# A hybrid decoder layer on one core: arithmetic moved off GpSimd, and another order of the branches S5, gMLP and SSD

## The chip, the core and the metric

The kernel runs on one core of a Trainium2 chip. The metric is device time in microseconds (us) of one execution, the median of several runs. The engines of the core are named as in the profile: PE is TensorE (PEld its weight loads), DVE is VectorE, ACT is ScalarE, POOL is GpSimd, SP is SyncE, which issues most of the DMAs.

## What is computed

One inference step of one layer for 256 prompt positions and 8 decode rows (264 columns in all), in float32. Cut to what matters here:

```python
mod = silu(c) @ w_mod + b_mod                       # 6 sections: shift, scale, gate, twice
h = rmsnorm(x, g_mix) * (1 + sc_m) + sh_m
u_a, u_b, v_b, z_c, xbc_c, dt_c, gates = split(h @ w_in)
o_a = s5_branch(u_a, ...)      # complex diagonal SSM: scan, Re(C h) + D u, gelu, y * sigmoid(y @ w_glu)
o_b = gmlp_branch(gelu(u_b), gelu(v_b), ...)        # u * (tril(w_s) @ rmsnorm(v) + b_s)
o_c = ssd_branch(z_c, xbc_c, dt_c, ...)  # conv(4), silu, chunked scan, rmsnorm(y * silu(z))
g_a, g_b, g_c = split(sigmoid(gates))
merged = g_a * (o_a @ w_pa) + g_b * (o_b @ w_pb) + g_c * (o_c @ w_pc)
x = x + gt_m * (merged @ w_out)
x = x + gt_f * conv_ffn(rmsnorm(x, g_ffn) * (1 + sc_f) + sh_f)   # up, conv(3), silu(a) * b, down
y = rmsnorm(x, g_final)
```

Beside y the states of S5, of SSD and of both convolutions are returned, for the prompt and for the decode rows, and gMLP's normalized v of the decode rows.

## The kernel before

Features lie on the 128 partitions, the 264 positions on the free axis. A weight matrix is streamed in pieces of 512 KB (128 x 1024 floats). `load_w` (line 287) loads one, ACT makes its rounded upper half `hi`, and DVE, or for some pieces POOL, subtracts it from the raw piece for the lower half `lo` (line 243). A product is three matmuls, hi times the input's upper and lower half and lo times the upper one; 24 matmuls use up a piece (`gemm_piece`). `prefetch` keeps three pieces ahead of PE. The sums of a group of 256 columns lie in one of three PSUM buffers (`PG`); S5's `read_in` takes two of the same three. Large tiles of activations, gates, tables and states share one pool of 24 buffers (`Q`, `Q1k`).

PE's program order is that of the stages: five K steps (`KSTEPS`), in which a fraction of K of all columns of xbc, S5's input, v, u, half of gMLP's gate and dt is multiplied and added on DVE into `acc` tiles; then the projections w_gb (rest of gMLP's gate), w_pb, w_ga, w_pa, w_z, w_gc, w_pc, w_out, and the feed-forward part in two halves (w_up0, w_down0, w_up1, w_down1). The modulation of the next K step is computed beside a K step (`mod_gen`, `mod_part`): matmuls of 32 output rows, so that four chunks of K can stand in PE's four column groups. The other sections of the modulation are spread over later stages (`mod_sec`, `mpump`).

The rest of the branches is written as generators: `gen_s5_prep`, `gen_s5_tables` (tables of cosines and sines by doubling), `gen_gm`, `gen_dt`, `gen_s5`, `gen_ssd` (convolution, then the chunked scan), `gen_ssd_dec` (eight decode rounds) and `gen_ssd_out`. They stand in a queue, `fill`. After each piece the projection calls `pump(pace)`: it adds `pace` to a credit and takes steps of the first generator until the credit is used up; a step's `yield` names its cost, and a `BRK` ends the turn. The queue before is gMLP, dt, S5, SSD; decode and output follow after w_z. `finish(g)` issues what is left of a generator at once, where its result is needed: gMLP ahead of w_pb, S5 ahead of w_pa, SSD ahead of w_gc, and the SSD output ahead of w_pc. The framework orders each engine's instructions by this program order and by when it expects their inputs to be ready, so that later work may go ahead of earlier work that waits.

The end: `residual` sums the squares of the new x while w_down1 is evacuated, `rstd_tok` makes the factor (six small DVE instructions and a diagonal `dg`, then a matmul `rsb`), and `final` multiplies and stores.

Of the kernel before, what the change touches and what calls it, by code (L numbers as in the profile page):

```python
# [30 lines left out]
SHARED = ("w_pb", "w_ga", "w_pa", "w_z")  # L31
# [35 lines left out]
def cuts(nk):  # L67

    n = 4 // nk
    out = [[DT]]  # L70
    for lo, hi in ((0, 6), (6, 12 + NGA)):
        out += [list(range(a, min(a + n, hi))) for a in range(lo, hi, n)]
    return out[1:] + out[:1]


def pack(i):
# [119 lines left out]
def build(tc, I, O):  # L196
# [62 lines left out]


# [26 lines left out]
    def load_w(src, kk, n, e=V):  # L287
# [5 lines left out]
        sub(lo, raw, hi.bitcast(F32), e)  # L293
# [64 lines left out]
    def mod_gen(s_, k0, nk, depth):  # L358
# [4 lines left out]
        for j in range(len(steps) + depth):  # L363
# [88 lines left out]
    def finish(g):  # L452
        while g in fill:
            try:
                next(fill[0])
            except StopIteration:
                fill.popleft()
# [32 lines left out]
    def rstd_tok(pt, PM=PM, n=D):  # L490
# [10 lines left out]
        ts(dg[:, :128], ident, r[:, 0:1], ALU.mult)  # L501
# [127 lines left out]
    def gen_s5_tables():  # L629
        co, si = trig[:, 0], trig[:, 1]  # L630
        tt = W("tt", [P, 512]).rearrange("p (a s m) -> p a s m", a=2, s=4)
        for u in range(4):
            tab = Q1k("tab").rearrange("p (a s t) -> p a s t", a=2, s=4)
            tc_, ts_ = tab[:, 0], tab[:, 1]
            tabs[u] = (tc_, ts_)
            V.memset(tc_[:, :, 0:1], 1.0)
            V.memset(ts_[:, :, 0:1], 0.0)
            e = G
            for b in range(7):
                m = 2 ** b  # L640
                cb = co[:, b, 4 * u:4 * u + 4].unsqueeze(2).to_broadcast([P, 4, m])
                sb = si[:, b, 4 * u:4 * u + 4].unsqueeze(2).to_broadcast([P, 4, m])
                t1, t2 = tt[:, 0, :, :m], tt[:, 1, :, :m]
                mult(t1, ts_[:, :, :m], sb, e)
                mult(t2, ts_[:, :, :m], cb, e)
                mult(tc_[:, :, m:2 * m], tc_[:, :, :m], cb, e)
                mult(ts_[:, :, m:2 * m], tc_[:, :, :m], sb, e)
                sub(tc_[:, :, m:2 * m], tc_[:, :, m:2 * m], t1, e)
                add(ts_[:, :, m:2 * m], ts_[:, :, m:2 * m], t2, e)
                yield 0.2  # L650
# [126 lines left out]
    def gen_gm(ub, vb):  # L777
# [29 lines left out]
        yield BRK  # L807
        d = W("gmd", [P, 4, NB])
# [87 lines left out]
    def gen_ssd(raws):  # L896
# [29 lines left out]

        tk, csd = xsb["tk"], xsb["csd"]
# [18 lines left out]
        act(CB, pt.rearrange("p (c g i) -> p c g i", c=2, g=2), AF.Copy)  # L946
        CBf = CB.rearrange("p c g i -> p (c g) i")
        G.affine_select(out=CBf, in_=CBf, compare_op=ALU.is_ge, fill=0.0, base=0,
                        pattern=[[0, 4], [1, 128]], channel_multiplier=-1)
# [73 lines left out]
    def gen_ssd_dec():  # L1023
        dd, bc, yv = xsb["dd"], xsb[2], xsb["yv"]
        E = Q1k("E")
        G.memset(E[:16, :], 1.0)
        G.affine_select(out=E[:16, :], in_=E[:16, :], compare_op=ALU.is_ge, fill=0.0, base=0,
                        pattern=[[1, 1024]], channel_multiplier=-64)
        G.affine_select(out=E[:16, :], in_=E[:16, :], compare_op=ALU.is_ge, fill=0.0, base=63,
                        pattern=[[-1, 1024]], channel_multiplier=64)  # L1030
# [136 lines left out]
    wsrc = W("wsrc", [P, 256], BF16)  # L1167
# [32 lines left out]
    for s_, (k0, nk) in enumerate(KSTEPS):  # L1200
        nxt = None
        if s_ + 1 < NS:
            nxt = step_mods(s_ + 1)
            mods.append(nxt)
            if s_ == 0:
                prefetch()
                mpump(DEPTH(1))
        if k0 == 8:
            fill.append(g_prep)
        if s_ == NS - 1:  # L1210
            fill.append(g_tab)
        for g, first, o in [(g, i == 0, 256 * i) for gs in cuts(nk) for i, g in enumerate(gs)]:
# [25 lines left out]
    finish(g_tab)  # L1238
# [41 lines left out]
    finish(g_gm)  # L1280
# [183 lines left out]
```

## Time and profile before

| | us |
|---|---|
| median of 3 timed runs | 1696.12 (1695.43 to 1696.61) |
| the profiled execution | 1694.82 |
| its span, first to last instruction | 1692.8 |
| PE busy in the span | 1641.0 |
| DVE / ACT / POOL busy | 1098.5 / 799.7 / 201.0 |

The profile is one execution. The busy time of an engine is the time in which at least one of its instructions runs; matmuls are pipelined, so that a busy PE is not PE at its peak. The clock of PE that the chip granted is given as a share of 2.4 GHz.

### The profile page before, as it was taken

How to read it: one execution, taken by the hardware profiler on the slowest of the kernel's cores; microseconds unless marked ns; L12 is line 12 of the kernel's file. 1: busy time of each engine (PE TensorE's matmuls, PEld its weight loads, DVE VectorE, ACT ScalarE, POOL GpSimd, SP SyncE). 2: the span in 40 equal slices, each digit the busy share in tenths (PEclk: the TensorE clock that was granted, in tenths of full speed). 3: DMA queues.
4: the chain of work that ended last, by engine and by line, in shares of the span. 5: the costliest groups of instructions: out<-in, count | busy, mean ns of one | idle time of the engine just before them, and what ended most of it. 6: DMA issues, size and time to landing. Idle time of an engine off the chain costs nothing.

```text
span 1692.8 us, 32239 instructions
## 1 busy us (share of the span) xinstructions
PE 1641.0 (97%) x13175; PEld 1515.9 (90%) x13175; DVE 1098.5 (65%) x1817; ACT 799.7 (47%) x1166; POOL 201.0 (12%) x252
## 2 busy tenths in 40 slices
PE   8999999989988999999999999999999999999996
PEld 6678899877967899879989999999999999999996
DVE  3456877599987658675547666666545566666554
ACT  4423346534345779644335444545333445455442
POOL 0200069133332320000000000000000000000000
PEclk8999999999999999999999999999999999999998
DMA  8867885766477659768996666555555555555552
GB/s 322 299 239 286 339 290 174 284 211 242 174 272 275 224 198 322 258 218 298 337 329 200 229 219 224 175 174 189 184 179 182 180 181 186 178 186 180 186 178 98
DMA packets 107268, 385.13 MB, mean 228 GB/s; under 512 B 12192, under 2 KB 13408, under 8 KB 107120
## 3 DMA queue, kind: packets, MB, share of 16 engines
q1 hardware_dynamic: 103968, 372.58, 63.1%
q0 software_dynamic: 3152, 10.50, 1.7%
q8 instruction: 103, 1.69, 0.4%
q14 instruction: 45, 0.37, 0.1%
HBM read 374.56 MB, written 8.46 MB: 226 GB/s over the span
## 4 chain that ended last, share of the span: by engine, by line
PE 86%; DVE 8%; DMA 2%; ACT 2%; issue 1%; SPq 0%; DVEq 0%; ACTq 0%
PE pg L258 79%; PE mods L258 3%; PE mod L258 2%; DVE lo L243 1%; DVE cv L246 1%; DVE s5b L237 1%; DVE s5gr L737 1%; ACT hi L255 1%; DMA raws<-in_w_mod 1%; DVE s5gi L737 1%; DMA raw<-in_w_pc 0%; DVE s5b L240 0%; DVE s5b L243 0%; PE ypy L258 0%; DMA cT<-in_c 0%
## 5 line engine op out<-in xcount | busy, mean ns | idle before, releaser
L243 DVE TENSOR_TENSOR lo<-raw,hi 128x1024 fp32r<-128x1024 f32 x457 | 568.1, 1244 | 418.6 <-ACT hi L255 401.8
L255 ACT ACTIVATE hi<-raw 128x1024 fp32r<-128x1024 f32 (+1 forms) x495 | 520.4, 1054 | 647.0 <-PE pg L258 495.5
L258 PE MATMUL pg<-hh,hi 128*128 128x264 f32 x1408 | 399.5, 284 | 0.0
L258 PE MATMUL pg<-hh,lo 128*128 128x264 f32 x1408 | 399.3, 284 | 0.0
L258 PE MATMUL pg<-hl,hi 128*128 128x264 f32 x1408 | 398.4, 283 | 0.0
L258 PE MATMUL pg<-xh,hi 128*128 128x264 f32 x1296 | 373.9, 289 | 4.7 <-ACT xh L255 2.5
L258 PE MATMUL pg<-xh,lo 128*128 128x264 f32 x1296 | 369.7, 286 | 1.9 <-DVE lo L243 1.8
L258 PE MATMUL pg<-xl,hi 128*128 128x264 f32 x1296 | 369.0, 285 | 0.0
L258 PEld LDWEIGHTS pg<-xh,hi 128*128 128x128 f32 x1296 | 244.5, 189 | 37.5 <-issue 17.9
L258 PEld LDWEIGHTS pg<-hh,hi 128*128 128x128 f32 x1408 | 264.5, 188 | 10.9 <-issue 9.2
L258 PEld LDWEIGHTS pg<-hl,hi 128*128 128x128 f32 x1408 | 264.4, 188 | 0.0
L258 PEld LDWEIGHTS pg<-hh,lo 128*128 128x128 f32 x1408 | 264.3, 188 | 0.0
L258 PEld LDWEIGHTS pg<-xh,lo 128*128 128x128 f32 x1296 | 243.9, 188 | 8.6 <-issue 4.8
L258 PEld LDWEIGHTS pg<-xl,hi 128*128 128x128 f32 x1296 | 244.4, 189 | 5.2 <-issue 4.9
L258 PE MATMUL pg<-fl,hi 128*128 128x264 f32 x704 | 199.6, 284 | 0.0
L258 PE MATMUL pg<-fh,hi 128*128 128x264 f32 x704 | 199.4, 283 | 0.0
L258 PE MATMUL pg<-fh,lo 128*128 128x264 f32 x704 | 199.3, 283 | 0.0
L258 PEld LDWEIGHTS pg<-fh,hi 128*128 128x128 f32 x704 | 132.4, 188 | 0.0
L258 PEld LDWEIGHTS pg<-fh,lo 128*128 128x128 f32 x704 | 132.4, 188 | 0.0
L258 PEld LDWEIGHTS pg<-fl,hi 128*128 128x128 f32 x704 | 132.3, 188 | 0.0
L243 POOL TENSOR_TENSOR lo<-raw,hi 128x1024 fp32r<-128x1024 f32 x38 | 99.6, 2622 | 274.9 <-ACT hi L255 230.9
L246 DVE SCALAR_TENSOR_TENSOR fcv<-pg,par,fcv 128x255 f32<-128x255 f32 (+1 forms) x176 | 83.9, 477 | 1.5 <-ACT fcv L255 1.5
(346 smaller groups left out, 1990.9 us busy)
## 6 DMA issues: line engine op xcount, KB each, us to landing
raw<-in_w_up SPq DMA_DIRECT2D x176, 512.0 KB, 3.5
raws<-in_w_mod SPq DMA_DIRECT2D x128, 512.0 KB, 5.9
raw<-in_w_down SPq DMA_DIRECT2D x88, 512.0 KB, 3.5
raw<-in_w_a SPq DMA_DIRECT2D x64, 512.0 KB, 5.2
rawm<-in_w_m SPq DMA_DIRECT2D x64, 512.0 KB, 7.0
raw<-in_w_ga SPq DMA_DIRECT2D x32, 512.0 KB, 3.8
raw<-in_w_gc SPq DMA_DIRECT2D x32, 512.0 KB, 5.0
raw<-in_w_out SPq DMA_DIRECT2D x32, 512.0 KB, 4.6
```

Source lines behind the costliest of these rows:

```text
L237: e.tensor_tensor(o, a, b, op=ALU.mult)
L243: e.tensor_tensor(o, a, b, op=ALU.subtract)
L246: V.scalar_tensor_tensor(o, a, s, b, op0=op0, op1=op1)
L255: S.activation(o, a, f, **kw)
L258: TE.matmul(o, l, r, start=start, stop=stop, skip_group_check=True, **kw)
L737: V.tensor_tensor_scan(g[:, s, k], rb, b[:, s, k], ini[:, 4 + r, s:s + 1] if c else 0.0, op0=ALU.mult, op1=ALU.add)
```

## The change

- The K steps' and some projections' `lo` subtractions that POOL did go to DVE. S5's tables are made on DVE, with four instructions in place of six for each doubling. The triangular masks of gMLP and of SSD's C·B become multiplications by a constant `tri` on DVE; the expansion of the decode factors uses 2 matmuls with a masked operand instead of 16 with a 0/1 matrix from POOL. POOL keeps its DMAs and two multiplications of the last normalization.
- The last K step takes its groups in another order: v, u, dt, xbc, S5's input, gates. In it gMLP and dt are paid by a second queue, `side`, one turn per piece, and the convolution, now `gen_conv`, starts behind xbc's last group. `gen_s5_prep` and `gen_s5_tables` are put into the queue one K step earlier.
- The queue `fill` is convolution, then (once `side` is empty) S5, SSD, decode, output. w_z is projected ahead of w_pa. w_gc pays 2.2 a piece instead of 1.6.
- Two chunks of a modulation piece are multiplied in reverse order of their transfers.
- In `rstd_tok` ACT makes the first third of `dg`. At the end 12 matmuls without a use stand behind the last sums; the last two squares are added before they are summed; the factors are read from PSUM by DVE, and x is stored in eight parts.

```diff
-SHARED = ("w_pb", "w_ga", "w_pa", "w_z")
...
-def cuts(nk):
-
-    n = 4 // nk
+def cuts(s):
+
+
+    if s == len(KSTEPS) - 1:
+        return [[g] for g in (8, 9, 10, 11, DT, 0, 1, 2, 3, 4, 5, 6, 7, *range(12, 12 + NGA))]
+    n = 4 // KSTEPS[s][1]
...
-        sub(lo, raw, hi.bitcast(F32), e)
+        sub(lo, raw, hi.bitcast(F32))
...
-                for p_, raw in enumerate(got.popleft()):
+                for p_, raw in reversed(list(enumerate(got.popleft()))):
                     mod_part(sec, i + p_, nk, raw)
...
+    side = deque()
+
     def pump(us):
+
+
         credit[0] += us
+        while side:
+            try:
+                c = next(side[0])
+                if c is BRK:
+                    break
+                credit[0] -= c
+            except StopIteration:
+                side.popleft()
         while fill and credit[0] > 0:
...
+    def alone():
+
+        while side:
+            yield BRK
...
-        ts(dg[:, :128], ident, r[:, 0:1], ALU.mult)
+        act(dg[:, :128], ident, AF.Copy, scale=r[:, 0:1])
...
-            e = G
             for b in range(7):
                 m = 2 ** b
-                cb = co[:, b, 4 * u:4 * u + 4].unsqueeze(2).to_broadcast([P, 4, m])
-                sb = si[:, b, 4 * u:4 * u + 4].unsqueeze(2).to_broadcast([P, 4, m])
-                t1, t2 = tt[:, 0, :, :m], tt[:, 1, :, :m]
-                mult(t1, ts_[:, :, :m], sb, e)
-                mult(t2, ts_[:, :, :m], cb, e)
-                mult(tc_[:, :, m:2 * m], tc_[:, :, :m], cb, e)
-                mult(ts_[:, :, m:2 * m], tc_[:, :, :m], sb, e)
-                sub(tc_[:, :, m:2 * m], tc_[:, :, m:2 * m], t1, e)
-                add(ts_[:, :, m:2 * m], ts_[:, :, m:2 * m], t2, e)
-                yield 0.2
+                cb, sb = (v[:, b, 4 * u:4 * u + 4].unsqueeze(1).unsqueeze(3).to_broadcast([P, 2, 4, m])
+                          for v in (co, si))
+                t, new = tt[:, :, :, :m], tab[:, :, :, m:2 * m]
+                mult(t, tab[:, :, :, :m], sb)
+                mult(new, tab[:, :, :, :m], cb)
+                sub(new[:, 0], new[:, 0], t[:, 1])
+                add(new[:, 1], new[:, 1], t[:, 0])
+                yield (0.7, 0.7, 0.7, 0.8, 0.9, 1.2, 1.7)[b]
...
-        G.affine_select(out=w3, in_=w3, compare_op=ALU.is_ge, fill=0.0, base=0,
-                        pattern=[[0, 8], [1, 128]], channel_multiplier=-1)
-        bs = W("bs", [P, 4, 128])
-        nc.sync.dma_start(bs, I["bs"])
+        mult(w3, w3, tri.unsqueeze(1).to_broadcast([P, 8, 128]))
...
-        for t in range(8):
-            mm(pe[:, 16 * t:16 * t + 16], E[:16, 128 * t:128 * t + 128], ddf, True, True)
+        for o in range(2):
+            mm(pe[64 * o:64 * o + 64, :128], ones[:16, :64], ddm[:, o].rearrange("p t c -> p (t c)"), True, True,
+               tile_position=(0, 64 * o))
...
-            e = G if (i % 2 == 1 if nk == 1 else i % 3 == 1 and nk == 2) else V
...
-            e = G if i % 2 == 1 and name in SHARED else V
...
-    for name in ("w_gb", "w_pb", "w_ga", "w_pa", "w_z", "w_gc", "w_pc", "w_out", "w_up0", "w_down0", "w_up1", "w_down1"):
+    for name in ("w_gb", "w_pb", "w_ga", "w_z", "w_pa", "w_gc", "w_pc", "w_out", "w_up0", "w_down0", "w_up1", "w_down1"):
...
+        if k0 == 4:
+            fill.append(g_prep)
         if k0 == 8:
-            fill.append(g_prep)
+            fill.append(g_tab)
         if s_ == NS - 1:
-            fill.append(g_tab)
+            finish(g_tab)
...
+            if s_ == NS - 1:
+                if g == 11:
+                    g_gm = gen_gm(acc[5], acc[4])
+                    side.append(g_gm)
+                if g == DT:
+                    side.append(gen_dt(acc_dt))
+                if g == 5:
+                    fill.append(gen_conv(acc[:3]))
             pump(0.3 * nk)
...
-    g_s5, g_gm = gen_s5(acc[3]), gen_gm(acc[5], acc[4])
-    g_ssd = gen_ssd(acc[:3])
-    fill.extend([g_gm, gen_dt(acc_dt), g_s5, g_ssd])
+    g_s5, g_ssd = gen_s5(acc[3]), gen_ssd()
+    zs = []
+    g_so = gen_ssd_out(zs)
+    fill.extend([alone(), g_s5, g_ssd, gen_ssd_dec(), g_so])
...
-    project("w_z", Xk, KD, 4, epi_z, PACE, 0.5)
-    finish(g_ssd)
-    g_sd = gen_ssd_dec()
-    g_so = gen_ssd_out(zs)
-    fill.extend([g_sd, g_so])
-    gc = gates("w_gc", 1.6, 0.0)
+    gc = gates("w_gc", PACE, 0.0)
...
-                if end:
-                    sum_tok(sst[0], [t[:, 0, :]], False, j0 == 1)
+                if not end:
+                    add(ssq, ssq, t)
+                elif j0 == 0:
+                    t0 = t
                 else:
-                    add(ssq, ssq, t)
+                    add(t, t, t0)
+                    sum_tok(sst[0], [t[:, 0, :]], False, True)
...
+    wps = PG()
+    with tc.issue_after(newest(TE)):
+        for _ in range(12):
+            mm(wps[:, 0, :256], wsrc[:, :128], wsrc, True, True)
     rs = rstd_tok(sst[0])
-
-    def final(q, js, r, e):
+    rsb = W("rsb", [P, T])
+    act(rsb, rs, AF.Copy)
...
     final(1, h0, rsb, G)
     final(0, h1, rs, V)
-    final(2, slice(0, 4), rsb, V)
+    final(2, h0, rs, V)
+    final(2, h1, rs, V)
     final(1, h1, rsb, G)
...
+    final(3, h0, rs, V)
+    final(3, h1, rs, V, True)
```

## Rows read from the trace of the kernel before

**Rows 1.** The page, busy us of each engine, share of the span, instructions:

```profile
PE 1641.0 (97%) x13175; PEld 1515.9 (90%) x13175; DVE 1098.5 (65%) x1817; ACT 799.7 (47%) x1166; POOL 201.0 (12%) x252
```

**Rows 2.** Stages: from:to length, busy (x) of PE, PEld, DVE, ACT, POOL; clock, DMA, GB/s:

```profile
107.50:169.70 62.20, 61.14 (x470) 51.12 (x470) 38.85 (x62) 21.92 (x27) 0.00 (x0) 1.00 0.82 304
169.70:229.00 59.30, 59.30 (x478) 51.40 (x477) 50.97 (x143) 24.09 (x31) 4.70 (x24) 1.00 0.88 325
229.00:277.00 48.00, 48.00 (x399) 48.00 (x398) 34.37 (x37) 25.34 (x27) 48.00 (x104) 1.00 0.69 230
277.00:335.80 58.80, 58.80 (x497) 52.89 (x495) 36.54 (x61) 29.29 (x35) 25.23 (x45) 1.00 0.70 245
335.80:373.00 37.20, 32.97 (x242) 28.01 (x241) 31.52 (x61) 14.39 (x25) 10.66 (x5) 0.91 0.63 216
373.00:510.40 137.40, 129.59 (x1011) 106.47 (x1010) 122.17 (x200) 52.84 (x84) 46.39 (x18) 0.98 0.64 234
510.40:555.50 45.10, 39.38 (x288) 33.10 (x286) 37.23 (x64) 27.99 (x40) 12.34 (x8) 0.92 0.72 261
...
618.20:728.40 110.20, 102.78 (x813) 97.48 (x811) 77.86 (x89) 81.20 (x179) 7.54 (x14) 0.97 0.77 264
```

**Rows 3.** PE's waits: waiting line <- releaser: us in total, times, longest:

```profile
PE rsb L258 <- DVE dg L250: 8.9, 2, 7.0
...
PE pg L258 <- DVE gate L237: 3.6, 1, 3.6
PE pg L258 <- ACT xh L255: 2.5, 1, 2.5
PE pg L258 <- ACT s5b L255: 2.4, 1, 2.4
PE pg L258 <- ACT gate L255: 2.1, 1, 2.1
PE pg L258 <- DVE acc L237: 1.8, 1, 1.8
```

**Rows 4.** DVE from 373 to 510 us by form: count | busy us, mean ns | idle before:

```profile
L243 DVE TENSOR_TENSOR lo<-raw,hi 128x1024 fp32r<-128x1024 f32 x18 | 26.3, 1465 | 6.3 <-ACT hi L255 6.3
L737 DVE TENSOR_TENSOR_SCAN s5gr<-s5sm,s5ini,s5b 128x128 f32<-128x128 f32 x12 | 12.0, 1003 | 0.0
...
L240 DVE TENSOR_TENSOR hds<-hds,s5b 128x16 f32<-128x16 f32 x12 | 6.6, 573 | 1.6 <-ACT s5b L255 1.6
...
L240 DVE TENSOR_TENSOR s5b<-s5b,s5gi 128x512 f32<-128x512 f32 x6 | 6.3, 1049 | 0.0
L737 DVE TENSOR_TENSOR_SCAN s5gr<-s5sm,s5b 128x128 f32<-128x128 f32 x12 | 4.9, 407 | 0.0
...
L237 DVE TENSOR_TENSOR s5gr<-s5gr,tab 128x512 f32<-128x512 f32 x7 | 4.8, 681 | 0.0
```

**Rows 5.** The whole execution: POOL's and DVE's subtraction, a 16-column multiply:

```profile
L243 DVE TENSOR_TENSOR lo<-raw,hi 128x1024 fp32r<-128x1024 f32 x457 | 568.1, 1244 | 418.6 <-ACT hi L255 401.8
...
L243 POOL TENSOR_TENSOR lo<-raw,hi 128x1024 fp32r<-128x1024 f32 x38 | 99.6, 2622 | 274.9 <-ACT hi L255 230.9
...
L237 DVE TENSOR_TENSOR rd<-pg,mod 128x16 f32<-128x16 f32 x22 | 3.6, 165 | 0.0
```

**Rows 6.** PE in order of time, modulation alone, from 76 us: start, us:

```profile
76.51 1.07 PE L258 MATMUL mod<-rawm,cs 128*32 128x512 f32 x8
79.68 1.05 PE L258 MATMUL mod<-rawm,cs 128*32 128x512 f32 x4
```

**Rows 7.** DVE in order of time at 61 us, beside a POOL subtraction:

```profile
61.14 2.35 DVE L237 TENSOR_TENSOR hd<-x,gs 128x16 f32<-128x16 f32 x1
```

**Rows 8.** PE from 618 to 630 us by form:

```profile
L258 PE MATMUL dde<-dd,E 16*128 16x16 f32 x16 | 2.0, 259 | 0.0
```

**Rows 9.** ACT from 618 to 715 us by form:

```profile
L255 ACT ACTIVATE hi<-raw 128x1024 fp32r<-128x1024 f32 x31 | 32.6, 1056 | 19.9 <-DMA raw<-in_w_gc 14.5 <-PE pg L258 4.7 <-DMA raw<-in_w_pc 0.5
...
L255 ACT ACTIVATE hup<-BC,dx 128x128 f32<-128x128 f32 x64 | 20.1, 393 | 0.0
```

**Rows 10.** DVE in order of time, the tail:

```profile
1683.85 4.18 DVE L237 TENSOR_TENSOR x<-x,rsb 128x528 f32<-128x528 f32 x3 [0.46 <-ACT rsb L255]
```

More of the change, by code (lines that the diff above doesn't have):

```diff
@@ L258, in mm, with newest @@
         TE.matmul(o, l, r, start=start, stop=stop, skip_group_check=True, **kw)
+    def newest(e):
+        return next(i for i in reversed(nc.cur_bb.bb.instructions) if i.engine == e.engine)
     ident = cst.tile([P, P], F32, name="ident")
@@ L333, in mod_part @@
     def mod_part(sec, i, nk, raw):
-        if i == 0:
-            mod_ps[sec] = PM("mod")
-        ps = mod_ps[sec]
+        if sec not in mod_ps:
+            mod_ps[sec] = PM("mod"), [0] * 4
+        ps, seen = mod_ps[sec]
         for j in range(8 // nk):
@@ L450, in pump, with finish @@
             credit[0] = 0.0
-    def finish(g):
-        while g in fill:
+    def finish(g, line=None):
+        line = fill if line is None else line
+        while g in line:
             try:
-                next(fill[0])
+                next(line[0])
             except StopIteration:
-                fill.popleft()
+                line.popleft()
+    def alone():
+        while side:
+            yield BRK
     mods = deque()
@@ L945, in gen_ssd @@
         yield BRK
[L946 to L949, printed above, removed]
+        mult(CB.rearrange("p c g i -> p (c g) i"), pt.rearrange("p (c i) -> p c i", c=4),
+             tri.unsqueeze(1).to_broadcast([P, 4, 128]))
         yv = [Q("yv"), Q("yv")]
@@ L1024, in gen_ssd_dec @@
         dd, bc, yv = xsb["dd"], xsb[2], xsb["yv"]
[L1025 to L1030, printed above, removed]
+        ddm = W("ddm", [16, 2, 8, 2 * NB])
+        ddf = dd.rearrange("p a b -> p (a b)")
+        for o in range(2):
+            mult(ddm[:, o], ddf.unsqueeze(1).to_broadcast([16, 8, 2 * NB]),
+                 ident[:16, o:16:2].unsqueeze(2).to_broadcast([16, 8, 2 * NB]))
         yield BRK
         pe = PM("dde")
-        ddf = dd.rearrange("p a b -> p (a b)")
-        for t in range(8):
-            mm(pe[:, 16 * t:16 * t + 16], E[:16, 128 * t:128 * t + 128], ddf, True, True)
+        for o in range(2):
+            mm(pe[64 * o:64 * o + 64, :128], ones[:16, :64], ddm[:, o].rearrange("p t c -> p (t c)"), True, True,
+               tile_position=(0, 64 * o))
         dx = cst.tile([P, 8, 2, NB], F32, name="dx")
@@ L1127, in build @@
         o = 0
-        for i, gs in enumerate(cuts(nk)):
+        for i, gs in enumerate(cuts(s_)):
             n = 128 if gs == [DT] else 256 * len(gs)
-            e = G if (i % 2 == 1 if nk == 1 else i % 3 == 1 and nk == 2) else V
-            queue.append((I[f"w_a{s_}"][o:o + P * nk * n].rearrange("(p n) -> p n", p=P), nk, n, e))
+            queue.append((I[f"w_a{s_}"][o:o + P * nk * n].rearrange("(p n) -> p n", p=P), nk, n))
             o += P * nk * n
@@ L1166, in build @@
     wps = PG()
-    wsrc = W("wsrc", [P, 256], BF16)
+    wsrc = cst.tile([P, 256], BF16, name="wsrc")
     V.memset(wsrc, 0.0)
@@ L1272, in gates @@
         return sl
-    g_s5, g_gm = gen_s5(acc[3]), gen_gm(acc[5], acc[4])
-    g_ssd = gen_ssd(acc[:3])
-    fill.extend([g_gm, gen_dt(acc_dt), g_s5, g_ssd])
+    g_s5, g_ssd = gen_s5(acc[3]), gen_ssd()
+    zs = []
+    g_so = gen_ssd_out(zs)
+    fill.extend([alone(), g_s5, g_ssd, gen_ssd_dec(), g_so])
     PACE = 2.2
     gb = gates("w_gb", PACE, 0.5, acc[6:], 8 - NGA)
-    finish(g_gm)
+    finish(g_gm, side)
     obh, obl = oA["b"]
@@ L1288, in build, with epi_z @@
     ga = gates("w_ga", PACE, 0.5)
+    def epi_z(g, src):
+        if g % 2 == 0:
+            zs.append(Q("z"))
+        act(zs[-1][:, 2 * (g % 2):2 * (g % 2) + 2, :], src, AF.Silu)
+    project("w_z", Xk, KD, 4, epi_z, PACE, 0.5)
     finish(g_s5)
@@ L1427, in build, with final @@
                 lambda k: (AH[(k + p0) // 4][:, k % 4, :], AL[(k + p0) // 4][:, k % 4, :]), np_, 8, epi_d, 0)
+    wps = PG()
+    with tc.issue_after(newest(TE)):
+        for _ in range(12):
+            mm(wps[:, 0, :256], wsrc[:, :128], wsrc, True, True)
     rs = rstd_tok(sst[0])
-    def final(q, js, r, e):
+    rsb = W("rsb", [P, T])
+    act(rsb, rs, AF.Copy)
+    def final(q, js, r, e, lone=False):
         v = x1[q][:, js, :]
         n = v.shape[1]
-        mult(v, v, r.unsqueeze(1).to_broadcast([P, n, T]), e=e)
+        if lone:
+            for j in range(js.start, js.stop):
+                stt(x1[q][:, j, :], x1[q][:, j, :], pv("g_final", 4 * q + j, 4 * q + j + 1), r, ALU.mult, ALU.mult)
+        else:
+            mult(v, v, r.unsqueeze(1).to_broadcast([P, n, T]), e=e)
         nc.sync.dma_start(O["y"][q].rearrange("p (j t) -> p j t", j=4)[:, js, :], v)
```

37 lines of the change are left out of this document (14 added, 23 removed).

## The prediction

> **What bounds the kernel now.** I read first the busy times of the engines: TensorE (PE) is busy 97% of the span, VectorE (DVE) 65%, ScalarE (ACT) 47%, GpSimd (POOL) 12% [rows 1]. So only PE's own work and PE's pauses set the time. Then I cut the span at the stages of the program [rows 2]; the reader should subtract PE's busy time from the length of each row. Up to 335.8 us PE has next to no pause. Then it loses 4.2 us in the projection w_pb (335.8 to 373.0), 7.8 us in w_ga and the wait for S5 behind it (to 510.4), 5.7 us in S5's GLU and w_pa (to 555.5), and 7.4 us in w_gc and the wait for the SSD output (618.2 to 728.4): **25.2 us**. The clock column of the same four rows adds something: the share missing from 1.00, doubled, times the length is the time at 1.2 instead of 2.4 GHz: 6.7, 5.5, 7.2 and 6.6 us, together 26 us. Where PE works in such a stretch it loses half of it, so 0 to 13 us; I take 9, since a pause comes first and work fills most of the rest. Last I read who ended PE's pauses [rows 3]: the longest, 7.0 us, is the normalization of the SSD output (dg); the next are the merge of a gate (3.6) and S5's own evacuations (2.4, 2.1, 1.8). The DVE columns tell why S5 is late: in w_ga DVE is busy 122.2 of 137.4 us. From 728 us on PE is busy all the time until the tail, and the change touches nothing there but the tail.
>
> **1. GpSimd's subtractions go to DVE.** One takes 2.62 us on POOL, the same on DVE 1.24 [rows 5] (w_ga's mean of 1.465 [rows 4] holds stretched ones). But POOL's work is not free for DVE. In w_ga the scan with a start value takes 1.003 us on average, the same shape without one 0.407; the 16-column add 0.573; a 512-column add 1.049, where an undisturbed 512-column multiply takes 0.681 [rows 4]. The plainest case is earlier: a 16-column multiply of 2.35 us [rows 7], against 0.165 for another 16-column multiply [rows 5]. Adding up what each form of w_ga takes above its undisturbed neighbour (25 forms, six shown) gives 27.7 us of delay around 18 POOL subtractions, 1.5 us each. Giving those 18 to DVE costs 18 x 1.24 = 22 us. DVE thus gains some 6 us in w_ga, and I book nothing on PE's path. The bounds are 0 (below nothing isn't excluded, but PE can't gain more there than the pauses already counted) and, if DVE got no delay back, +22.
>
> The Trainium skill (Perfetto Trace Analysis, Optimizing Scalar/DVE Operations) holds that offloading to GPSIMD may make sense when DVE is saturated, which speaks against this edit, and adds that the two share an SBUF read port, so that it might not help. By its first half the time would be 22 us longer; the rows just read side with its second half.
>
> **2. S5 opens the branches, z goes ahead of w_pa.** `pump` pays S5 out at 2.2 units a piece. S5 needs 94 units, and each BRK throws away what is left of a piece. By this bookkeeping S5 in the kernel before starts with the first piece of w_pb, and ends inside `finish(g_s5)`, behind the last piece of w_ga: the pauses before 519 us. After, gMLP and dt are paid in the last K step, the convolution ends in w_gb, S5 starts five to six pieces into w_gb and ends three pieces before the end of w_ga, and all of w_z lies between it and w_pa. The same bookkeeping ends the SSD output 13 pieces of 2.9 us ahead of w_pc, where it is unfinished now. So the four stages' pauses are released: **-25.2 - 9 = -34.2 us**.
>
> What is late next? **(a) DVE from 169.7 us on.** The tables cost DVE four times 28 instructions. Their sizes lie between 4 and 512 columns, so one costs 0.165 [rows 5] to 0.68 us [rows 4], 28 of them by their sizes about 6.7, all 27 us. Some 20 fall into the K step from 169.7, in place of 15 us of `gen_s5_prep`, which goes a step ahead, where DVE is busy 38.9 of 62.2 us [rows 2]. The rest, 6.5 us, is issued by `finish(g_tab)` in one go ahead of the last K step, whose sums and low halves queue behind it on DVE. Stage by stage DVE then has: K step from 169.7: 51 - 15 + 20 = 56; last K step 34.4 + 6.5 + 1.2 (mask) + 12 (gMLP) = 54; w_gb 16 x 1.24 + 4 (dt) + 16 (36 convolution steps of some 255 columns, about 0.43 each by the rows of 16 and 512) + 22 (1.9 of S5's eight pairs at 11.5, which is what w_ga's 122.2 leave without delays and subtractions, over 6.1 pairs) = 62; w_pb 8 x (1.24 + 0.70 for a merge of 528 columns) + 18 = 34. gMLP's 12 and dt's 4 are what 277.0 to 335.8 leaves of its 36.5 without 16 subtractions. The sum is 206 us against PE's 59 + 52 (48.0 and gMLP's matmuls) + 58 + 32 = 201. DVE can't be kept busy all the time: in w_ga it is busy 89%, in w_pb 85%. At 93% it needs 221. PE has up to three prefetched pieces, 8.7 us, as cover. So 0 to +20; I take **+9**.
>
> **(b) Evacuations of S5.** `read_in` still takes two of three PSUM buffers from the projections; 2.4 + 2.1 + 1.8 us of such pauses [rows 3] can come back at another place: 0 to +6, I take **+3**.
>
> **(c) The pool of 24 tiles.** During w_z now 8 tiles of normalized input, 4 merged gates, 4 gates of w_ga, 2 of S5's output and 3 of the convolution are held, 21; z takes 2 more. The SSD part wants six (csb twice, L, yv twice, hprev) and z's second tile has to wait until w_pa's merges give back a gate. Meanwhile z's last two groups hold two of three PSUM buffers. Some four groups of w_pa then wait about 1.3 us each for their merge: 0 to +10, I take **+5**, about what w_pa loses already.
>
> **(d) ACT in w_gc.** A decode round has 16 scalings; the eight rounds take 20.1 + 20.1 us (the second row is the like of the one shown), 5.0 each, plus a conversion of 1.05 for every piece [rows 9]. At the new pace a round is paid in two pieces: 7.4 us of ACT per 5.8 us of PE, eight times 1.6 = 13 us, of which prefetch hides 8.7. If (c) makes the SSD late instead, the end of w_gc pauses again. 0 to +11, I take **+3**.
>
> **3. K steps.** Two halves of a modulation piece use two of PE's four column groups each. Side by side, 8 instructions take 1.07 us; alone, 4 take 1.05 [rows 6]. Seven pairs (79.7 to 148.2 us) run apart. Taken in reverse, the later transfer is awaited first and both follow at once: 7 x 0.98 = 6.9; I take **-5.5** (0 to -7, as PE can be kept waiting for the later one). Without POOL's subtraction the multiply of rows 7 shrinks by 2.2 us, which stands in front of the 2.5 us that PE waits for xh [rows 3]; the first sum of squares is delayed alike. Their own subtractions now queue on DVE: together **-2.8** (0 to -5).
>
> **4. Small.** Sixteen instructions of dde, 2.0 us [rows 8], become two: **-1.4**. The tail: three DVE instructions take 4.18 us there beside POOL [rows 10]; with the factor read from PSUM and half pieces stored, **-1.5** (+1 to -2.5: the twelve idle matmuls stand ahead of the last one, and one added sum stands in the chain). The masks in place of POOL's, ACT's share of dg, bs loaded later: under 0.5 us, beside other work.
>
> **Sum.** The profiled execution took 1694.8 us (span 1692.8); the median of the timed runs is 1696.1, 1.3 more. 1694.8 - 34.2 - 5.5 - 2.8 - 1.4 - 1.5 = 1649.4; + 9 + 3 + 5 + 3 = 1669.4; as a median 1670.7, say **1671**.
>
> **The rivals.** *Everything stays covered*: DVE's lag never exceeds the prefetched pieces and ACT's neither; half of the +20 or less comes back: 1651 to 1661. For it speaks that DVE's 89% in w_ga cost PE few pauses inside that stage; against it the flush of 6.5 us.
> *The tile pool decides* (c): SSD can't start before w_pa's end, decode rounds fill w_gc and its end pauses as now (7.4 us), w_pa loses 10: 1671 + 7 + 5 + some 6 at low clock = about 1689.
> *The other side, DVE becomes the bound* from 169.7 to the end of w_pb. It decides once DVE can't be kept busier there than w_pb's 85%: 206 / 0.85 = 242, 41 us over PE's 201 in place of my 9; PE would then fall to the low clock in its pauses too, as now after its waits. 1671 + 32 = 1703. Against it: 89% already held for 137 us.
> *The edit of GpSimd gives DVE nothing back*: DVE has 22 us more in w_ga than I book, 1671 + 22 = 1693. The delays in [rows 4, 7] speak against it. The first half of the skill's rule above would have it so.
> *The change does not do what it says* (S5 still ends late): pauses stay, only part 3 and 4 are left, 1696 - 11 + 9 = 1694.
>
> **How the numbers follow.** Forecast, 1661 to 1684: 0.54. All covered: 0.20. Tile pool: 0.11. GpSimd edit or S5 still late, about 1693: 0.05. DVE bound, over 1700: 0.10. The range reaches from the lower bound of what is released to the pool case: 1651 to 1692, 0.85 less tails of 0.05. A measurement tells 0.2%, 3.4 us, from no change: faster below 1692.7: 0.85 and half of the 1693 case, less a little for the pool case, 0.84; same 0.06; slower 0.10.
>
> **What would show it.** Right: no pause of PE over 3 us between w_ga and w_pa nor ahead of w_pc; no DVE instruction of S5 above 1 us; modulation matmuls all in eights; PE's busy share of 169.7 to 373's stages at 95% or more. Wrong: PE pauses in the last K step and w_gb ended by DVE's sums or low halves (a); z's second evacuation late and w_pa's groups waiting for their merge (c); ACT full in w_gc with PE waiting for low halves (d).

## The result, and the profile after

The changed kernel takes 1677.2 us (median of 4 runs, 1675.1 to 1683.8) beside 1696.1 before: a ratio of 0.990, 95% interval 0.987 to 0.993. That is 18.8 us less. The forecast was 1671, the range 1651 to 1692. The profiled execution took 1679.1 us, 9.7 over the 1669.4 that the sum gave for one execution. The total is near; the parts of the sum are not.

The page of the changed kernel, busy us, share of the span and instructions of each engine (compare [rows 1]):

```profile
PE 1624.6 (97%) x13163; PEld 1511.4 (90%) x13163; DVE 1097.3 (65%) x1969; ACT 804.4 (48%) x1172; POOL 21.0 (1%) x41
```

The stages of the changed kernel, in the columns of [rows 2]: K step from 160.8, last K step, w_gb, w_pb, w_ga with S5's GLU inside, w_z, w_pa, and w_gc with the SSD output.

```profile
160.80:219.60 58.80, 58.80 (x470) 50.93 (x469) 51.32 (x132) 20.60 (x24) 0.00 (x0) 1.00 0.90 323
219.60:276.70 57.10, 55.22 (x451) 53.98 (x450) 53.23 (x114) 37.37 (x49) 1.42 (x2) 0.97 0.52 169
276.70:336.50 59.80, 58.87 (x477) 51.32 (x475) 51.33 (x107) 37.87 (x53) 1.07 (x2) 1.00 0.70 242
336.50:367.20 30.70, 29.70 (x240) 25.34 (x241) 30.52 (x65) 10.27 (x17) 0.00 (x0) 1.00 0.80 284
367.20:491.60 124.40, 124.40 (x1001) 108.21 (x1000) 92.11 (x163) 57.47 (x85) 2.18 (x4) 1.00 0.74 254
491.60:550.00 58.40, 58.40 (x481) 51.32 (x480) 25.20 (x31) 23.98 (x26) 0.00 (x0) 1.00 0.82 290
550.00:586.30 36.30, 30.85 (x236) 26.18 (x234) 24.75 (x39) 16.71 (x29) 1.08 (x2) 1.00 0.67 237
586.30:714.20 127.90, 107.51 (x857) 103.57 (x858) 89.31 (x106) 94.51 (x198) 7.47 (x14) 0.91 0.64 215
```

Who ended PE's pauses in the changed kernel (compare [rows 3]):

```profile
PE pg L260 <- ACT hi L257: 19.1, 1, 19.1
PE pg L260 <- DVE gate L239: 5.7, 6, 2.1
PE pg L260 <- DVE acc L242: 3.5, 1, 3.5
```

Subtract PE's busy time from each length, as before. The pauses of w_pb, w_ga and the GLU are gone but for 1.0 us. w_pa still loses 5.5 us, and w_gc loses 20.4 us where it lost 7.4. From w_pb to the end of w_gc PE idles 26.8 us; it was 25.2. So on balance no pause was released. PE's *busy* time fell instead, from 1641.0 to 1624.6 us. Part of that is the modulation, whose halves now run side by side (see the experiment on it). Laying the granted clock over PE's busy time shows another reason: from the last K step to w_pc PE worked 21.7 us at 1.2 GHz before and 10.2 us now. Half of the difference, 5.8 us, is saved time. The long pause costs the clock too:

```profile
622.20:646.10 23.90, 6.80 (x29) 6.50 (x30) 22.82 (x21) 23.87 (x70) 3.00 (x6) 0.50 0.77 268
```

The last column group says that the clock was 0.50 (1.2 GHz) for 23.9 us, but PE worked in only 6.8 of them, after the pause; ACT was busy in 22.8.

A second table goes by the first matmul of each stage; before and after, in us:

| | before | changed | difference | by the prediction's terms |
|---|---|---|---|---|
| four K steps to the last one | 197.8 | 189.4 | -8.4 | -8.3 |
| last K step to the end of w_ga and S5 | 290.2 | 272.0 | **-18.2** | about -5 |
| w_pa, w_z, w_gc | 209.3 | 222.6 | **+13.3** | about -10.5 |
| tail | 16.4 | 15.7 | -0.7 | -1.5 |

The last column splits the prediction's sum by place. About -5 is -4.2 - 7.8 - 0.6 (what of the 5.7 us lies ahead of w_pa), half of the 9 us of low clock, + 9 (a) + 3 (b). About -10.5 is -5.1 - 7.4, the other half of the clock, + 5 (c) + 3 (d) - 1.4 (dde). These two are wrong by 13 and by 24 us, with opposite signs. They are differences of two single profiles; a second profile of the changed kernel has 269.6 and 226.5 in place of 272.0 and 222.6.

What fills the 19.1 us is on ACT. ACT of the changed kernel in order of time (start, length, operation, count, idle time before and what ended it):

```profile
606.82 2.02 ACT L257 ACTIVATE hi<-raw 128x1024 fp32r<-128x1024 f32 x2 [6.00 <-DMA raw<-in_w_gc]
...
610.27 7.11 ACT L257 ACTIVATE hst<-hst,dx 128x128 f32<-128x128 f32 x24
619.86 9.45 ACT L257 ACTIVATE hup<-BC,dx 128x128 f32<-128x128 f32 x32 [2.48 <-DMA BC<-bcd]
629.22 1.84 ACT L257 ACTIVATE hst<-hst,dx 128x128 f32<-128x128 f32 x6
631.08 1.28 ACT L257 ACT_TABLE_LOAD   x1
632.37 0.61 ACT L257 ACTIVATE gate<-pg 128x528 f32<-128x528 f32 x1
632.88 2.43 ACT L257 ACTIVATE hup<-BC,dx 128x128 f32<-128x128 f32 x8
635.21 2.44 ACT L257 ACTIVATE hst<-hst,dx 128x128 f32<-128x128 f32 x8
637.55 1.99 ACT L257 ACTIVATE hi<-raw 128x1024 fp32r<-128x1024 f32 x2
```

Between 608.8 and 637.6 ACT converts no weight. It scales decode states, waits for the transfer BC, then does four rounds of `hup` at once. PE uses up its prefetched pieces until 619.6 and waits. And decode is late because the SSD scan is late:

```profile
L260 PE MATMUL ypy<-L,xdt x64: 272/273/324, 509.8 to 601.8; 128*64 128x128 f32 x64
```

This row groups the scan's matmuls, with their first and last start: four parts of 16. The first part runs at 509.8 us, in w_z; the second at 575.2, in w_pa; the last ends at 602, in w_gc. The evacuations of w_z's four groups show the same shortage that the prediction's (c) described:

```profile
L257 ACT ACTIVATE z<-pg x4: 591/611/612, 509.3 to 597.4; 128x528 f32<-128x528 f32 x4
```

The first two start at 509.3 and 523.6 us. The third and fourth, which fill z's second tile, start only at 592.1 and 597.4, though w_z ended at 550.0. Until then two of the three PSUM buffers hold z, and w_pa's groups wait for each other's merge (five of the six waits for `gate` above, 4.7 us).

### The profile page after: what moved, and what is told of

It reads as the page before. It is cut to its first block, busy times and chain, and to the rows that moved or that the text cites. A ratio compares the mean times of both kernels' runs of the same rounds, so it can differ in the third digit from the quotient of the medians.

```text
span 1677.4 us, 32131 instructions
## 1 busy us (share of the span) xinstructions
PE 1624.6 (97%) x13163; PEld 1511.4 (90%) x13163; DVE 1097.3 (65%) x1969; ACT 804.4 (48%) x1172; POOL 21.0 (1%) x41
## 4 chain that ended last, share of the span: by engine, by line
PE 85%; issue 7%; DVE 5%; DMA 2%; ACT 1%; SPq 0%; DVEq 0%; POOL 0%; POOLq 0%; ACTq 0%
PE pg L260 79%; PE mods L260 3%; PE mod L260 2%; DVE lo L245 1%; DMA cT<-in_c 0%; DMA wsT<-in_wsT 0%; PE s5py L260 0%; DMA csb<-csd 0%; DMA bcd<-bct 0%; DVE yd L1096 0%; DVE hup L239 0%; DVE hst L242 0%; DMA BC<-bcd 0%; PE ypy L260 0%; PE modT L358 0%
## 5 line engine op out<-in xcount | busy, mean ns | idle before, releaser
L245 DVE TENSOR_TENSOR lo<-raw,hi 128x1024 fp32r<-128x1024 f32 (+2 forms) x495 | 601.3, 1216 | 425.5 <-ACT hi L257 408.8
L257 ACT ACTIVATE hi<-raw 128x1024 fp32r<-128x1024 f32 (+2 forms) x495 | 520.0, 1053 | 694.7 <-PE pg L260 571.3
L260 PE MATMUL pg<-xh,hi 128*128 128x264 f32 x1296 | 377.9, 292 | 24.7 <-ACT hi L257 19.1
L260 PEld LDWEIGHTS pg<-xh,hi 128*128 128x128 f32 x1296 | 247.0, 191 | 60.9 <-ACT hi L257 25.2
L260 PE MATMUL pg<-mh,hi 128*128 128x264 f32 x256 | 73.1, 286 | 0.0
```

Source lines behind the costliest of these rows:

```text
L245: e.tensor_tensor(o, a, b, op=ALU.subtract)
L257: S.activation(o, a, f, **kw)
L260: TE.matmul(o, l, r, start=start, stop=stop, skip_group_check=True, **kw)
```

## Experiments on the late SSD scan

**w_pa ahead of w_z again.**

```diff
-    project("w_z", Xk, KD, 4, epi_z, PACE, 0.5)
     finish(g_s5)
...
     project("w_pa", lambda k: (oah[:, k, :], oal[:, k, :]), 4, 8, epi_a, PACE, 0.5)
+    project("w_z", Xk, KD, 4, epi_z, PACE, 0.5)
```

> The changed kernel with w_pa projected before w_z again (weights streamed in that order); nothing else differs. Theory Tiles: w_z ahead of w_pa leaves the SSD scan without tiles of the pool of 24 until w_pa gives gates back; the decode rounds behind it are already issued, come late all at once, and ScalarE's conversions for w_gc stand behind them, which is the 19.2 us pause of TensorE at 619 us. Then this kernel has the SSD scan done by the end of w_z, no pause over 4 us in w_gc, no row of 1 us waits in w_pa, and takes 1677 - 19 - 3 = about 1655 us (1650 to 1660). Theory Rate: ScalarE has too much to do in w_gc at the higher pay of 2.2 a piece, wherever the scan ends; then a pause of over 10 us stays in w_gc and the time is 1670 to 1680. If S5 is what w_pa waits for, there is a pause ahead of w_pa of up to 8 us and the time is about 1663.

Measured: 1656.1 us, ratio to the kernel before 0.976 (0.974 to 0.977). The scan's row now, and the stages w_pa, w_z, w_gc:

```profile
L260 PE MATMUL ypy<-L,xdt x64: 272/273/323, 503.7 to 549.3; 128*64 128x128 f32 x64
```

```profile
485.60:518.20 32.60, 32.60 (x278) 28.19 (x276) 27.85 (x43) 17.19 (x25) 1.08 (x2) 1.00 0.78 264
518.20:580.20 62.00, 62.00 (x522) 54.70 (x521) 32.78 (x51) 38.33 (x80) 3.76 (x7) 1.00 0.82 296
580.20:690.30 110.10, 99.17 (x778) 96.53 (x778) 78.14 (x83) 73.15 (x143) 3.74 (x7) 0.98 0.69 235
```

The scan ends at 549 us, w_pa has no pause, and the three stages take 204.7 us instead of 222.6. The last two groups of w_z are evacuated at 569.1 and 586.5 us, within 7 us of the end of w_z. This is the number of theory Tiles. There is no wait for S5 ahead of w_pa, so z in front of it hid nothing. Pauses of 10.9 us in all are left in w_gc, one of 3.9 us ahead of the sum `css`, the others of 1.4 us at most. So not all of theory Tiles' list came: w_gc's longest pause is just under the 4 us that it allowed, and the small waits have moved there.

**Decode put into the queue only behind w_pa**, z still ahead.

```diff
-    fill.extend([alone(), g_s5, g_ssd, gen_ssd_dec(), g_so])
+    fill.extend([alone(), g_s5, g_ssd])
...
+    finish(g_ssd)
+    fill.extend([gen_ssd_dec(), g_so])
     gc = gates("w_gc", PACE, 0.0)
```

> The changed kernel, with w_z still ahead of w_pa, but decode and SSD output put into the queue behind w_pa and a finish of the SSD scan, as before the change. The scan still lacks tiles. Theory Early issue: the pause arises because decode is issued before its inputs can exist; then it is gone, w_pa keeps its 5 us of waits for merges, and the time is 1655 to 1663 us. Theory Tiles alone: the scan itself is what is late, so decode starts no sooner than now (about 606 us) and the SSD output is late instead: a pause of 10 to 20 us at the end of w_gc, ahead of w_pc, and 1670 to 1680 us. The flush of the scan at the end of w_pa may itself cost a pause of a few us there.

Measured: 1664.6 us (0.981, 0.979 to 0.983). The scan is as late as in the changed kernel (its last part at 594 to 597 us), yet the long pause is gone; ACT alternates between decode and conversions:

```profile
606.25 1.06 ACT L257 ACTIVATE hi<-raw 128x1024 fp32r<-128x1024 f32 x1 [0.23 <-DMA raw<-in_w_gc]
607.22 1.85 ACT L257 ACTIVATE hst<-hst,dx 128x128 f32<-128x128 f32 x6
608.97 1.05 ACT L257 ACTIVATE hi<-raw 128x1024 fp32r<-128x1024 f32 x1
609.92 1.85 ACT L257 ACTIVATE hst<-hst,dx 128x128 f32<-128x128 f32 x6
611.67 1.05 ACT L257 ACTIVATE hi<-raw 128x1024 fp32r<-128x1024 f32 x1
```

So two things act. The late scan alone costs w_pa 5.4 us and moves SSD work into w_gc; the 19 us come only when decode has been issued ahead of inputs that can't be there, and so stands in ACT's order ahead of the conversions. The Trainium skill (Perfetto Trace Analysis, Tensor Engine Instruction) says that ACT, DVE and GpSimd take their instructions strictly in order; the trace of the changed kernel agrees: ACT stands idle 2.5 us ahead of `hup` until 619.9 us, and no conversion passes it, though the transfers of the next three pieces had been issued by 610.3 us and such a piece lands some 5 us later. In the 28.7 us without a conversion ACT mostly works; it is the order of the work that keeps PE waiting.

**The old pay in w_gc**, `gates("w_gc", 1.6, 0.0)` in place of 2.2.

> The changed kernel with w_gc paying 1.6 a piece to the queue, as before the change. Theory Rate (term d of the prediction): two pieces a decode round are too few for ScalarE; with three the pause of 19.2 us shrinks below 6 and the time is 1658 to 1664 us. Theories Tiles and Early issue: the first rounds are issued in w_pa and w_gc's first pieces and come when their inputs come; the pause stays over 10 us and the time is 1670 to 1680 us.

Measured: 1673.5 us (0.986, 0.984 to 0.989). The pause is 14.3 us instead of 19.1, still over 10:

```profile
PE pg L260 <- ACT hi L257: 14.3, 1, 14.3
```

The lower rate alone does not remove the pause, and at the high rate it is gone in the two runs above; the rate only thickens what stands ahead of the conversions.

**Two more tiles.** `pool("qp", 26)`, `pool("rm", 5)`.

> The changed kernel with 26 instead of 24 tiles in the large pool, paid with 5 instead of 7 buffers for the modulation's weights and decode states. Theory Tiles: with two tiles more the scan goes on in w_z, z's second tile comes in time, the five waits of about 1 us in w_pa and the pause in w_gc are gone: w_pa and w_gc together shorter by 20 to 25 us. Theory Rate or Early issue without tiles: these two stages stay within 5 us. The K steps up to 277 us may lose up to 10 us for want of modulation buffers, which is read apart from this; so 1653 to 1668 us by Tiles, 1677 to 1688 us otherwise.

Measured: 1684.4 us (0.991, 0.989 to 0.994), not what theory Tiles expected. Here the second part of the scan comes in w_z (at 528 us instead of 575), but the two last ones only at 586 and 598 us:

```profile
PE pg L260 <- ACT hi L257: 10.4, 1, 10.4
PE pg L260 <- DVE gate L239: 6.1, 4, 3.7
```

The pause shrinks to 10.4 us, w_pa and w_gc together to 158.3 from 164.2 us; w_z takes 62.6 instead of 58.4, and the steps ahead of it lose some 3 us. So two tiles carry the scan one part further, as a shortage of tiles would have it; they are not enough: z's second tile still comes late (592.8 and 598.0 us, w_z ending at 557.7). More were not tried. That w_z first leaves the scan without tiles is made likely by the first experiment together with this one; which allocation waits for which tile was not shown.

## Experiments on GpSimd's subtractions

**Given back to GpSimd** in the changed kernel.

```diff
-        sub(lo, raw, hi.bitcast(F32))
+        sub(lo, raw, hi.bitcast(F32), e)
...
-            queue.append((I[name][i], nk, 256))
+            queue.append((I[name][i], nk, 256, G if i % 2 == 1 and name in SHARED else V))
```

> The changed kernel with the low halves that GpSimd had made before (every second piece of w_pb, w_ga, w_pa, w_z and every third of the first two K steps) given back to GpSimd. Theory Delay (the prediction's): GpSimd's subtractions delay DVE by about as much as they spare it; in w_ga DVE's busy time changes from 92 us by less than 6, S5's scans are stretched again to 1 us and more, and the time stays within 4 us of the changed kernel plus some 2 us in the K steps: 1675 to 1684 us. Rival Offload: DVE is spared 16 x 1.24 = 20 us in w_ga and goes to 75 us or below there; PE can gain little in w_ga, where it has no pause, but the SSD and w_pa gain and the time falls below 1672. Rival Pressure: the freed time on DVE was what let S5 end in time, and without it a pause over 4 us comes back ahead of w_z or w_pa: above 1684.

The changed kernel beside it took 1676.9 us (0.989, 0.987 to 0.991); what had been expected of that run:

> The changed kernel as it is, beside the next three on one chip. Its pause in w_gc and the waits in w_pa should be there again (19 and 5.5 us), with the time 1675 to 1684 us. Profiles so far differ by up to 6 us in when the first K step begins (26.0 to 32.0 us), in the same code; if that is the execution and not the program, the start here need not be 30.3 us.

With the subtractions on GpSimd it took 1688.5 us (0.995, 0.993 to 0.997), **11.6 more**. That is the number of rival Pressure, but not its place: the pause over 4 us stands in the middle of w_ga, not ahead of w_z or w_pa. Theory Delay was right on DVE and wrong on the time. In w_ga DVE is no less busy for 16 subtractions fewer: about 93 us in 126, where the changed kernel has 92.1 in 124.4. As the prediction had it, the delays eat what is spared. DVE from 370 to 496 us by form, with GpSimd's subtractions, beside [rows 4]:

```profile
L246 DVE TENSOR_TENSOR lo<-raw,hi 128x1024 fp32r<-128x1024 f32 x18 | 24.9, 1385 | 12.7 <-ACT hi L258 12.7
L759 DVE TENSOR_TENSOR_SCAN s5gr<-s5sm,s5ini,s5b 128x128 f32<-128x128 f32 x8 | 7.8, 979 | 0.0
L243 DVE TENSOR_TENSOR hds<-hds,s5b 128x16 f32<-128x16 f32 x8 | 6.6, 848 | 0.9 <-ACT s5b L258 0.9
```

The same forms in the changed kernel:

```profile
L758 DVE TENSOR_TENSOR_SCAN s5gr<-s5sm,s5ini,s5b 128x128 f32<-128x128 f32 x8 | 3.8, 473 | 0.0
L242 DVE TENSOR_TENSOR hds<-hds,s5b 128x16 f32<-128x16 f32 x8 | 1.2, 170 | 0.1
```

The loss is in what a delay does to others. One case, from three engines of this run (POOL, DVE, ACT) in order of time:

```profile
409.83 2.58 POOL L246 TENSOR_TENSOR lo<-raw,hi 128x1024 fp32r<-128x1024 f32 x1 [6.29 <-ACT hi L258]
```

```profile
410.13 2.55 DVE L759 TENSOR_TENSOR_SCAN s5gi<-s5sm,s5ini,s5b 128x128 f32<-128x128 f32 x1
```

```profile
416.84 0.19 ACT L716 COPY s5po<-s5b 128x2 f32<-128x2 f32 x1 [7.09 <-DVE s5b L243]
416.94 0.59 ACT L258 ACTIVATE mev<-mods 128x512 f32<-128x512 f32 x1
417.44 0.19 ACT L716 COPY s5po<-s5b 128x2 f32<-128x2 f32 x1
417.54 2.00 ACT L258 ACTIVATE hi<-raw 128x1024 fp32r<-128x1024 f32 x2
419.45 0.59 ACT L258 ACTIVATE gate<-pg 128x528 f32<-128x528 f32 x1
```

The scan, 0.47 us elsewhere, takes 2.55 while GpSimd subtracts. ACT stands 7.1 us, 2.1 of them for the held scan, at a copy of two columns that needs S5's next product. Behind it in ACT's order are two conversions and the evacuation of `gate` from PSUM, and for that PE waits 4.5 us, and then works 6.1 us at 1.2 GHz. w_ga takes 133.2 us instead of 124.4. DVE's busy time shows nothing of this. ACT's idle time at these copies (`s5po`, ten of them in w_ga) does. With GpSimd's subtractions, 23.4 + 6.6 = 30.0 us:

```profile
  DVE s5b L243: 23.4, 5
  DVE s5b L246: 6.6, 2
```

The changed kernel without them, 6.7 + 2.7 = 9.4 us:

```profile
  DVE s5b L242: 6.7, 4
  DVE s5b L245: 2.7, 5
```

Where nobody waits for DVE, the subtractions cost nothing: GpSimd makes eight of w_z's low halves in this run, and w_z takes 58.4 us with them as without.

**Taken from GpSimd in the kernel before**, by one line and nothing else.

```diff
-        sub(lo, raw, hi.bitcast(F32), e)
+        sub(lo, raw, hi.bitcast(F32))
```

> The kernel before, with GpSimd's subtractions of low halves given to DVE and nothing else (the tables and masks stay on GpSimd). Prediction: 2.8 us in the first K steps, nothing on PE's path later, about 1693 us. Theory of the run before (giving them back to GpSimd cost the changed kernel 11.6 us, of which 8.8 in w_ga): a DVE instruction held for 2 us by GpSimd makes ScalarE wait in its order, and evacuations of PSUM behind it; then w_pb, w_ga and w_pa lose pauses here too, 6 to 14 us in all, and the time is 1682 to 1690 us. Rival Offload: S5 ends behind w_ga here, and DVE, busy 122 of 137 us in w_ga, gets 22 us more to do; the wait ahead of w_pa grows and the time is over 1700 us.

Measured: **1667.8 us** (0.983, 0.982 to 0.984), 27.7 less than before, and 9 less than the whole change. All three expectations were too small or on the wrong side. Its stages w_pb, w_ga (with S5's end) and w_pa:

```profile
329.10:359.60 30.50, 30.06 (x241) 25.73 (x241) 28.61 (x53) 13.84 (x23) 0.55 (x1) 1.00 0.73 251
359.60:495.40 135.80, 133.43 (x1072) 110.97 (x1071) 116.81 (x234) 58.55 (x90) 1.12 (x2) 1.00 0.73 265
495.40:526.00 30.60, 30.14 (x232) 24.56 (x231) 29.38 (x63) 21.59 (x34) 2.18 (x4) 1.00 0.92 322
```

Against the stages of before w_pb takes 6.6 us less, w_ga with S5's end 10.3, w_pa 5.9: 22.8. Another 5.2 come from the first three K steps. S5 still begins in w_pb and ends behind w_ga. In these three stages PE's pauses fall from 17.8 to 3.3 us, and the clock is 1.00 throughout, where [rows 2] has 0.91, 0.98 and 0.92. ACT's idle time at its sixteen copies `s5po` falls from 43.9 to 23.2 us.

Both edits crossed, by the time from the last K step to the end of w_ga and S5:

| | low halves partly on GpSimd | all on DVE |
|---|---|---|
| S5 late (kernel before) | 290.2 | 273.1 |
| S5 early (changed kernel) | 279.6 | 272.0 (269.6 in the second profile) |

The rows of this table differ by all the rest of the change, S5's early start among it; no run has the early start alone. GpSimd's edit alone brings 17.1 us, the rest alone 10.6, both together 18.2 to 20.6. After GpSimd's edit the rest is worth only 1 to 4 us here, little more than the 2.4 us between two profiles of one kernel (the convolution lies within this time only where S5 is early; it is work of DVE and ACT).

**The reversed modulation alone**, in the kernel before.

> The kernel before, with part 3 of the prediction alone: two chunks of a modulation piece are multiplied in reverse order of their transfers. Theory (prediction): seven pairs that ran apart, 0.98 us each, run side by side, so the K steps up to 229 us are 5.5 us shorter (0 to 7) and the time is about 1690 us. Rival: PE only waits for the later transfer instead, and the K steps keep their length; 1696 us.

Measured: 1687.0 us (0.995, 0.994 to 0.996), 8.5 less. The first three K steps take 130.9 us instead of 138.5, and all modulation from 69 us on runs in eights. A pause of 3.6 us is new, at the end of the second K step, as in the changed kernel:

```profile
PE pg L258 <- DVE acc L240: 3.6, 1, 3.6
```

The three steps take 133.3 us with GpSimd's edit alone and 130.6 with both. These two do not add either.

## A kernel faster than both

With w_pa first and 1.6 a piece in w_gc:

> w_pa ahead of w_z again, and w_gc pays 1.6 a piece instead of 2.2. With w_pa first, 10.9 us of pauses were left in w_gc: 4.05 ahead of the sum css, the rest small waits for hi and lo. Theory Spread: the rounds of decode that w_gc pays are too dense for ScalarE and DVE (term d of the prediction), so with 1.6 the pauses fall below 6 us and the time is 5 us lower than with w_pa first alone (1650 to 1653 us, by the earlier runs). Theory Burst: the pauses come from the first four rounds, issued in w_z; then nothing changes by over 2 us. If the SSD output ends too late, a pause ahead of w_pc of up to 8 us comes back.

Measured: **1652.5 us** (0.975, 0.972 to 0.977), 43 less than before. w_gc has 3.2 us of pauses left, and the three stages take 195.0 us:

```profile
582.50:682.90 100.40, 97.18 (x778) 96.07 (x777) 77.18 (x81) 72.00 (x139) 3.73 (x7) 0.98 0.74 258
```

Beside the run with w_pa first alone the medians differ by 3.6 us and the ratios by less than their intervals; the stage w_gc, 100.4 instead of 110.1 us, shows the gain better. The SSD output ends 10 us ahead of w_pc, and the 7.0 us wait of [rows 3] is gone, as it is in the changed kernel; in the kernel before with GpSimd's edit alone, which has the same order of projections, 6.8 us of it are left. So it is here that the earlier start of the branches seems to pay, but no run has it alone. A version with more turns ahead of decode and of `css` gave the same:

> w_pa ahead of w_z again, w_gc pays 2.0, four more turns are passed before the first decode round and two more before the sum css. The aim is a kernel without pauses in w_gc: the rounds then begin when their inputs are there, and PE does not reach css before DVE. If that is all that is left, 6 to 9 us less than with w_pa first alone: 1647 to 1650 us; if the pauses come from ScalarE's total work, 1653 to 1657.

Measured: 1653.8 us (0.975, 0.973 to 0.977), w_gc 104.9 us with 4.4 us of pauses. The number is that of the alternative, ScalarE's total work (1653 to 1657), not the 1647 to 1650 that was aimed at; the pauses in w_gc fell from 10.9 us nevertheless, and the wait at `css` is gone. This run changes the rate and the turns at once, so what each of them brings is not shown; together they bring no more than the lower rate did.

## Why the prediction was right or wrong

**Released pauses, -34.2: half of them came, and they were booked to the wrong edit.** Up to the GLU the pauses went as forecast (12.6 us, of which 1.0 is left). The 12.5 us of w_pa and w_gc did not go; the changed kernel has 25.8 there. Of the 9 us for the low clock 5.8 came back. And the prediction booked all of it to the new order, S5's early start above all, and nothing to part 1. Part 1 alone, in the kernel before, gave 27.7 us.

**Part 1, "nothing on PE's path": wrong, by 11.6 us with S5 early and 27.7 with S5 late** (5.2 of these in the K steps, where part 3 had booked 2.8 for them). The step that failed is the inference from DVE's busy time. Its arithmetic held (16 subtractions cost what the delays give back). But PE does not wait for DVE's sum, it waits for single links: a scan held for 2 us, ACT behind it in its order, an evacuation behind that. "PE can't gain more there than the pauses already counted" was true and was the trap: the pauses had been counted under another part, which beside this one brought only 1 to 4 us up to the end of w_ga.

**(a) DVE from the K step at 160.8 us: too dear.** +9 was taken. The four stages to the end of w_pb take 206.4 us, with 3.8 us of pauses and a stretch at 0.97 of the clock; a second profile has 203.9. The term that was mis-sized is DVE's work: 206 us were added up, 186.4 measured, 11 of the difference in w_gb (62 against 51.3). DVE is busy 90% of the time: it can be kept busier than the 85% from which the rival of a DVE bound would have decided. Of the 13 us by which these stages came out better than the forecast, (a) and (b) explain 8 (12 taken, 3.8 us of pauses measured); for the rest no cause was found. In the last K step 1 to 2 us of wait stand ahead of gMLP's sum `vss`; whether the flush of the tables causes it was not tried.

**(b) S5's evacuations: +3 taken, 1.0 measured**, at 355 us, where PE waits behind `read_in` until a merge gives back the third buffer.

**(c) The tile pool: mechanism, place and size right in w_pa, its consequence in w_gc missed.** Both signs that the prediction named came: z's second evacuation is late, and w_pa's groups wait for their merge (5.5 us; +5 was taken). That the late scan would push decode, all at once, in front of w_gc's conversions was not seen: the prediction's (d) weighed only the rate of decode. This is the step that failed by most: +3 was taken on top of 7.4 released, and w_gc's pauses grew from 7.4 to 20.4 us. (By the rows that (d) names, ACT's work for two pieces is 5.0 + 2 x 1.05 = 7.1 us, not 7.4; the difference does not matter beside this.) Together w_z ahead of w_pa cost 18 us by the stages, and the medians of the two runs differ by 21. The rival "tile pool decides" named the cause but priced it at 18 over the forecast; it came true, and GpSimd's edit paid for it.

**Part 3, -5.5 - 2.8: the sum right, -8.4 measured.** The two overlap: alone they give 7.6 and 5.2 (by the first three K steps).

**Tail, -1.5: -0.7**, and 16.2 instead of 16.4 in the second profile. The three multiplications beside POOL [rows 10] became five of together 3.2 us, but the chain ahead of them kept its length.

```profile
1667.92 3.16 DVE L239 TENSOR_TENSOR x<-x,rsb 128x528 f32<-128x528 f32 x5 [1.29 <-ACT rsb L257]
```

**The time came out inside the range by luck: two errors of 13 and 24 us met**, one in each direction.

## What to carry to other kernels

- Price an offload to GpSimd by the chain that runs through the delayed instruction, not by DVE's busy time: find the instruction it overlaps, who waits for that in order, and what stands behind the waiting one.
- Before a projection is moved ahead of another one, count which of them takes buffers and which gives them back, and follow what the held work will issue when it comes late: decode that was queued early on ACT blocked the weight conversions behind it.
- When one pause has two edits that could remove it, their gains need not add (17.1 and 10.6 us gave 18 to 21 here); only each edit alone tells which one is worth having.

## What the runs showed of the hardware

- A GpSimd subtraction of two inputs (2.4 to 2.6 us) holds a DVE instruction with both inputs in SBUF that starts behind its start, until it ends, whatever the size of the held one. In the run with the subtractions given back the five held scans end 0.28 us behind the subtraction's end, the four held 16-column adds 0.03 to 0.04; a scan took 2.55 instead of 0.47 us, and the mean of a 16-column add rose from 0.17 to 0.85. The merges `gate<-gate,pg`, which read one input from PSUM, are not held: four started beside a subtraction in that run and took 0.69 to 0.70 us.
- The first K step's matmuls began between 26.0 and 32.0 us after the span's start in the profiles; the changed kernel alone shows 30.3 and 27.4, and its last K step took 57.1 and 54.6 us. So a difference of 3 us between single executions of two kernels shows nothing by itself.
- In the changed kernel a pause of 3.5 us between the second and the third K step is followed by 3.4 us of work at 1.2 GHz (5.9 in another run with the same pause), and the pause of 19.1 us by 6.8. Here the long pause cost little more in clock than the short one.
